# Down projections of a gated FFN by Strassen's seven block products, with written orders on three engines

## The chip, the cores and the metric

One Trainium2 chip, of which the kernel uses one core. Inside the core, TensorE multiplies matrices (a 128 x 128 block of weights is loaded, then up to 512 columns stream through it into a bank of PSUM), VectorE and GpSimd do elementwise work, ScalarE does activations and copies, and DMA queues move data between HBM and SBUF (here mostly the queue of SyncE). Only VectorE and ScalarE read PSUM here; GpSimd works on SBUF alone.

The metric is the device time of one execution in microseconds, as the median of the runs. Before the change it is 1626.29 us over three runs (1626.14 to 1626.61).

## The reference, cut to what matters

A trunk of two layers on 512 tokens with 1024 features: layer 0 mixes by dilated attention, layer 1 by a state space scan, and each is followed by the same gated FFN with 2816 hidden features. The change touches only the last product of the FFN:

```
def conv_ffn(h, w_up, conv_w, conv_b, w_down):
    u = causal_depthwise_conv(h @ w_up, conv_w, conv_b)
    gate, up = u[..., :D_FF], u[..., D_FF:]
    return (jax.nn.silu(gate) * up) @ w_down

for i in range(DEPTH):
    ...
    h = rmsnorm(x, ffn_norm_w[i])
    x = x + conv_ffn(h, ffn_w_up[i], ffn_conv_w[i], ffn_conv_b[i], ffn_w_down[i])
```

## The kernel before

**Layout and precision.** Features lie on the 128 partitions, tokens along the free dimension. The residual stream is eight tiles `xr[0..7]` of 128 x 512. Every operand of a large product is split into a high part (a cast to fp32r, on ScalarE) and a low part (value minus high part, on VectorE for weights, on GpSimd for the gated operands). `mm3` (line 136) then issues three products into one bank of PSUM: high weights by high operand, high by low, low by high. `in_turns` (line 129) only permutes the order in which columns stream.

**Loading.** `load_unit` (line 116) brings one 128 x 1024 block of weights: one DMA of 512 KB on SyncE's queue into a `raw` buffer (a ring of 4), the cast into `hi` (ScalarE), the difference into `lo` (VectorE). `hi` and `lo` have rings of 5, so units are prepared up to four ahead of TensorE.

**The FFN** (`ffn`, line 610) runs in three parts of 8, 8 and 6 tiles of hidden features (`FF_PARTS`). In each part an **up stage** goes over the tiles `c`. For the gate and the up half (`i = 2c`, `2c + 1`), `project` (line 146) makes 24 products of 512 columns into one of three `mm` banks; VectorE scales the bank by the row norm into `us` (line 620); `conv` (line 602) starts the three-tap convolution on ScalarE and adds two taps on VectorE. Then ScalarE takes the Silu of the gate half, GpSimd multiplies the halves (line 627), ScalarE casts the product and GpSimd takes the difference (line 630).

The **down block** follows: `down` (line 263) goes over the eight output tiles `m`; each has `cn` column blocks of weights in one loaded unit and `3 cn` products of 512 columns in one bank, after which VectorE adds the bank to `xr[m]` (line 640). The products that need the last hidden tile are put off (`held`, `late`), so that its convolution and split have time. Part 2 of layer 1 ends in `finish` (line 1059) instead, with the final norm; its last two output tiles are computed in halves of 256 tokens.

**What sets the order.** The scheduler of the framework orders each engine's instructions from a simulated timeline, except inside `tc.manual_schedule(engines=...)`: there the listed engines issue the block's instructions in the order of the program text. Where these fall among the same engine's instructions of outside the block stays with the scheduler. Before the change only TensorE's order is written in the down blocks. Other names that the steps below use: `aux_bank` (three banks of PSUM) and `side_bank` (two), `rbc` (the row norm along the free dimension), and `lp` and `k2`, the pools of SBUF tiles whose `tag` names a ring of buffers.

Of the kernel before, what the change touches and what calls it, by code (L numbers as in the profile page):

```python
# [51 lines left out]
def trunk(ctx: ExitStack, tc: tile.TileContext, A, out):  # L52
# [23 lines left out]
    def t2(name, tag, bufs, pool=k2, dtype=F32):  # L76
        return pool.tile([P, 512], dtype, tag=tag, name=name, bufs=bufs)
# [51 lines left out]
    def in_turns(ap):  # L129

        return ap.rearrange("p (a b f) -> p b a f", b=4, f=4)

    def long_product(dst, w, x, first, last):
        T.matmul(in_turns(dst), w, in_turns(x), start=first, stop=last)  # L134

    def mm3(dst, hi, lo, at, rh, rl, first, last):
        w_h = hi[:, at * P : (at + 1) * P]
        w_l = lo[:, at * P : (at + 1) * P]
        long_product(dst, w_h, rh, first, False)
        long_product(dst, w_h, rl, False, False)  # L140
        long_product(dst, w_l, rh, False, last)

    loaded = {}
    early = {}
# [457 lines left out]
    def conv(dst, src, c_w, c_b, taps):  # L602
        SC.activation(dst, src, AF.Identity, bias=col(c_b), scale=col(c_w + taps - 1))  # L603
        for j in range(1, taps):
            V.scalar_tensor_tensor(  # L605
                dst[:, j:], src[:, : S - j], col(c_w + taps - 1 - j), dst[:, j:],
                op0=ALU.mult, op1=ALU.add,
            )

    def ffn(layer, done):  # L610
        for part, (c0, cn) in enumerate(FF_PARTS):
            gh, gl = [], []
            for c in range(c0, c0 + cn):
                ab = []
                for gu in range(2):
                    i = 2 * c + gu
                    n = f"u{layer}_{i}"
                    p = project(A["wup"][layer * 44 + i], n)
                    us = t2("us" + n, "us", 3, lp)
                    V.tensor_tensor(us, p, rbc, op=ALU.mult)  # L620
                    a = t2("a" + n, "a", 13, lp)
                    conv(a, us, C_FCW + (layer * 44 + i) * 3, C_FCB + layer * 44 + i, 3)
                    ab.append(a)
                SC.activation(ab[0], ab[0], AF.Silu)

                by = V if layer == 1 and c == NFF - 1 else G
                by.tensor_tensor(ab[1], ab[0], ab[1], op=ALU.mult)  # L627
                g_h, g_l = high_low(f"g{c}")
                SC.copy(g_h, ab[1])
                by.tensor_tensor(g_l, ab[1], g_h.bitcast(F32), op=ALU.subtract)  # L630
                gh.append(g_h)
                gl.append(g_l)
            n = cn * P

            def load(m):
                i = (layer * len(FF_PARTS) + part) * KD + m
                return (*load_unit(A["wdn"][i][:, :n], f"wd{i}", n), 0)

            def add(m, p):
                V.tensor_tensor(xr[m], xr[m], p, op=ALU.add)  # L640
                if part == len(FF_PARTS) - 1:
                    done(m)

            if layer == 1 and part == len(FF_PARTS) - 1:
                finish(load, lambda c: (gh[c], gl[c]), cn)
                return
            with tc.manual_schedule(engines={mybir.EngineType.PE}):
                down(f"wd{layer}{part}", load, range(KD), lambda c: (gh[c], gl[c]), cn, add, late=True)

    def ups(layer, some):  # L650
        return [(A["wup"][layer * 44 + i], f"u{layer}_{i}") for i in some]
# [524 lines left out]
def _layout(i):  # L1176

    a = {k: np.asarray(v) for k, v in i.items()}
    f = np.float32
    xt = a["x"].reshape(S, D).T  # L1180
    xp = xt.reshape(D, P, DIL).transpose(0, 2, 1).reshape(KD, P, S)
    w = {"xt": xt.reshape(KD, P, S), "xp": xp}
    qkv = a["attn_w_qkv"][0].reshape(KD, P, NG, 3, NH, HD)
    qk = qkv[:, :, :, :2].transpose(4, 2, 3, 1, 0, 5).reshape(NH, 6, P, D)
    v0 = qkv[:, :, 0, 2].transpose(2, 1, 0, 3).reshape(NH, 1, P, D)
    w["wqk"] = np.concatenate([qk, v0], 1).reshape(56, P, D)
    w["wv"] = (
        qkv[:, :, 1:, 2].reshape(4, 2, P, 2, 2, 512).transpose(3, 4, 0, 2, 1, 5).reshape(16, P, D)
    )
# [5 lines left out]
    wdn = np.zeros((2, len(FF_PARTS), KD, P, 8, P), f)  # L1195
    for part, (c0, cn) in enumerate(FF_PARTS):
        wdn[:, part, :, :, :cn] = dn[:, c0 : c0 + cn].transpose(0, 3, 2, 1, 4)
    w["wdn"] = wdn.reshape(-1, P, 1024)
# [24 lines left out]
    return w  # L1223
# [22 lines left out]
```

## Time and profile before

| | |
|---|---|
| median of 3 runs | 1626.29 us (1626.14 to 1626.61) |
| the profiled execution | 1626.55 us |
| its span in the profile | 1624.6 us |
| mean granted clock of TensorE | 0.999 |
| read from HBM over the span | 161.62 MB |

The profile comes from one execution, so sums made from its rows stand against 1626.55 us. Its views name engines by short names: PE is TensorE, PEld its loads of weights, DVE VectorE, ACT ScalarE, POOL GpSimd, SP or SPq the queue of SyncE. A row of a group gives the source line, engine, operation, output and inputs by the names of the program, shapes and count, then total busy time and mean duration, then the idle time of the engine just before these instructions and what ended it. A row of the timeline gives the start in us from the start of the span, the duration, and the instruction. Matmuls are pipelined: the duration of one is longer than the distance from one to the next, which is what counts. Busy time of an engine is no limit of itself; it must be read stage by stage.

### The profile page before, as it was taken

The page shows a single profiled execution, that of the slowest core. Times are in us where ns is not written, and L with a number is a line of the kernel's source. Part 1 is how long each engine was busy: PE and PEld are TensorE (multiplying, and loading weights), DVE is VectorE, ACT ScalarE, POOL GpSimd, SP SyncE. Part 2 cuts the span into 40 slices and gives each one's busy share as a digit, 9 for nine tenths or more (in the row PEclk, how much of TensorE's full clock was granted, in tenths as well). Part 3 has the DMA queues.
Part 4 walks back from the last instruction along what each step waited for, and adds up shares of the span by engine and source line. Part 5 has one row for each costly group of instructions (what it writes and reads, how often), then busy time and mean ns, then how long its engine had stood idle before and what let it go on. Part 6 is the DMA issues. An engine that isn't in the chain of part 4 may idle for free.

```text
span 1624.6 us, 21067 instructions
## 1 busy us (share of the span) xinstructions
PE 1615.7 (99%) x8038; PEld 1382.9 (85%) x8038; DVE 1082.8 (67%) x1813; ACT 655.0 (40%) x965; POOL 418.6 (26%) x272
## 2 busy tenths in 40 slices
PE   9999999999999999999999999999999999999998
PEld 8888888888888888888887888888888888888887
DVE  6366665266647855764657899988897784574564
ACT  5233332333334532432445455544443442342343
POOL 0444453045402320220231222222111341121020
PEclk9999999999999999999999999999999999999999
DMA  7322222222224323223233433334332232332321
GB/s 259 98 80 83 78 91 80 96 85 79 78 78 134 113 91 105 103 81 117 81 101 104 148 108 115 100 100 127 114 126 90 93 104 91 104 104 91 104 78 52
DMA packets 53235, 165.13 MB, mean 102 GB/s; under 512 B 6224, under 2 KB 9680, under 8 KB 53136
## 3 DMA queue, kind: packets, MB, share of 16 engines
q1 hardware_dynamic: 52304, 163.01, 30.5%
q8 instruction: 63, 1.03, 0.3%
q10 hardware_dynamic: 832, 0.79, 0.1%
q14 instruction: 36, 0.29, 0.1%
HBM read 161.62 MB, written 2.16 MB: 101 GB/s over the span
## 4 chain that ended last, share of the span: by engine, by line
PE 99%; ACT 0%; DVE 0%; POOL 0%; POOLq 0%; DVEq 0%; issue 0%
PE u L134 29%; PE qk L134 16%; PE wd L134 12%; PE v L134 8%; PE xs L134 5%; PE z L134 5%; PE wso L134 5%; PE wo L134 3%; PE c L134 3%; PE b L134 3%; PE wz L134 2%; PE py L830 1%; PE pg L490 1%; PE pp L477 1%; PE po L485 1%; PE pf L838 1%
## 5 line engine op out<-in xcount | busy, mean ns | idle before, releaser
L134 PE MATMUL u<-xh,lo_u 128*128 128x512 f32 x704 | 268.9, 382 | 0.0
L134 PE MATMUL u<-xh,hi_u 128*128 128x512 f32 x704 | 268.8, 382 | 0.0
L134 PE MATMUL u<-xl,hi_u 128*128 128x512 f32 x704 | 266.3, 378 | 0.0
L627 POOL TENSOR_TENSOR au<-au,au 128x512 f32<-128x512 f32 x43 | 58.5, 1360 | 422.2 <-DVE au L605 396.6
L605 DVE SCALAR_TENSOR_TENSOR au<-usu,par,au 128x511 f32<-128x511 f32 (+1 forms) x176 | 159.4, 911 | 7.6 <-ACT au L603 2.9
L125 ACT CAST hi_u<-raw_u 128x1024 fp32r<-128x1024 f32 x88 | 91.1, 1044 | 168.4 <-PE u L134 95.6
L388 POOL TENSOR_TENSOR rotqk<-rotqk,sr 32x512 f32<-32x512 f32 x48 | 88.2, 1837 | 250.2 <-DVE rotqk L387 239.8
L134 PEld LDWEIGHTS u<-xl,hi_u 128*128 128x128 f32 x704 | 131.7, 187 | 24.5
L134 PEld LDWEIGHTS u<-xh,lo_u 128*128 128x128 f32 x704 | 131.7, 187 | 24.0
L134 PEld LDWEIGHTS u<-xh,hi_u 128*128 128x128 f32 x704 | 131.7, 187 | 21.8 <-issue 0.4
L134 PE MATMUL qk<-xh,hi_qk 128*128 128x512 f32 x384 | 148.6, 387 | 0.0
L134 PE MATMUL qk<-xh,lo_qk 128*128 128x512 f32 x384 | 147.1, 383 | 0.0
L134 PE MATMUL qk<-xl,hi_qk 128*128 128x512 f32 x384 | 145.6, 379 | 0.0
L126 DVE TENSOR_TENSOR lo_u<-raw_u,hi_u 128x1024 fp32r<-128x1024 f32 x88 | 113.8, 1299 | 29.9 <-ACT hi_u L125 29.9
L620 DVE TENSOR_TENSOR usu<-u,rbc 128x512 f32<-128x512 f32 x88 | 60.3, 690 | 93.1 <-PE u L134 86.4
L640 DVE TENSOR_TENSOR xr<-xr,wd 128x512 f32<-128x512 f32 x40 | 27.3, 688 | 116.9 <-PE wd L134 116.9
L125 ACT CAST hi_qk<-raw_qk 128x1024 fp32r<-128x1024 f32 x48 | 50.3, 1047 | 130.3 <-PE qk L134 69.3
L134 PEld LDWEIGHTS qk<-xh,lo_qk 128*128 128x128 f32 x384 | 71.8, 187 | 13.3
L134 PEld LDWEIGHTS qk<-xl,hi_qk 128*128 128x128 f32 x384 | 71.9, 187 | 12.8
L389 POOL TENSOR_TENSOR qk<-qk,rotqk 32x512 f32<-32x512 f32 x48 | 81.5, 1698 | 3.8
L125 ACT CAST hi_wd<-raw_wd 128x1024 fp32r<-128x1024 f32 (+1 forms) x48 | 46.1, 972 | 88.7 <-PE wd L134 55.6
L134 PEld LDWEIGHTS qk<-xh,hi_qk 128*128 128x128 f32 x384 | 71.9, 187 | 11.2
(647 smaller groups left out, 3768.5 us busy)
## 6 DMA issues: line engine op xcount, KB each, us to landing
raw_u<-in_wup SPq DMA_DIRECT2D x88, 512.0 KB, 3.3
raw_qk<-in_wqk SPq DMA_DIRECT2D x48, 512.0 KB, 3.3
raw_wd<-in_wdn SPq DMA_DIRECT2D x32, 512.0 KB, 3.2
raw_xs<-in_win SPq DMA_DIRECT2D x16, 512.0 KB, 3.3
raw_z<-in_win SPq DMA_DIRECT2D x16, 512.0 KB, 3.4
lm<-rows SPq DMA_DIRECT2D x32, 256.0 KB, 5.4
raw_wso<-in_wso SPq DMA_DIRECT2D x16, 512.0 KB, 3.3
raw_v<-in_wv SPq DMA_DIRECT2D x12, 512.0 KB, 3.5
```

What stands on the lines that cost most here:

```text
L125: SC.copy(hi[:, s], raw[:, s])
L126: low.tensor_tensor(lo[:, s], raw[:, s], hi.bitcast(F32)[:, s], op=ALU.subtract)
L134: T.matmul(in_turns(dst), w, in_turns(x), start=first, stop=last)
L388: G.tensor_tensor(rot[R, :], rot[R, :], sr[R, :], op=ALU.mult)
L389: G.tensor_tensor(at(t)[R], at(t)[R], of(rot)[R], op=ALU.add)
L477: T.transpose(pp[:, b * P : (b + 1) * P], pr[:, b * P : (b + 1) * P], ident)
L485: T.matmul(po[:, ii], v0[h][:, b * P : (b + 1) * P], pts[i][:, (b - i + 1) * P : (b - i + 2) * P], start=b == max(i - 1, 0), stop=b == i,)
L490: T.matmul(pg[:, ii], vt[g, half][i][:, es], pts[i][:, (g + 1) * P : (g + 2) * P], start=g == 1, stop=g == 2,)
L605: V.scalar_tensor_tensor(dst[:, j:], src[:, : S - j], col(c_w + taps - 1 - j), dst[:, j:], op0=ALU.mult, op1=ALU.add,)
L620: V.tensor_tensor(us, p, rbc, op=ALU.mult)
L627: by.tensor_tensor(ab[1], ab[0], ab[1], op=ALU.mult)
L640: V.tensor_tensor(xr[m], xr[m], p, op=ALU.add)
```

## The change

In parts 0 and 1 of both layers the down block is computed by a form of Strassen's scheme with 15 additions. The eight hidden tiles are taken in four pairs, the eight output tiles in four pairs (`mp`), the 512 tokens in two halves `H0` and `H1`. Instead of eight block products per pair, seven are made, with sums of weight blocks (`load_sevens`: `sums`, then `split_weights` of `a`, `b`, `c` with 1024 columns each and `d` with 512) and sums of operand halves (`split_first`, `split_second`, on GpSimd). Each block product is 128 x 128 by 256 columns, with the three products of `mm3` as before.

The results of the products are put together through `s1`, `s5`, `u`, `v` by ScalarE copies, VectorE adds from PSUM and GpSimd adds. Weights of the next row pair are prepared during the present one. Ahead of the block stand the two projections of the next part's first hidden tile (the **cover**, `held`): TensorE runs them while the last operands are split. The orders of TensorE, VectorE and ScalarE are written from the cover to the end of the block. Part 2 keeps the old block (its weights are laid out without padding now). The core of the diff:

```diff
+    def split_first(c, ga):
+        y = t2(f"y{c}", "a", 13, lp)
+        G.tensor_tensor(y[:, H0], ga[:, H1], ga[:, H0], op=ALU.subtract)
+        h, l = high_low(f"g{c}")
+        split_by(G, h[:, H0], l[:, H0], ga[:, H0])
+        split_by(G, h[:, H1], l[:, H1], y[:, H0])
+        return y, (h, l)
+    def split_second(c, ga, gb, y, j, fourth):
+        x = t2(f"x{c}", "a", 13, lp)
+        G.tensor_tensor(x[:, H0], gb[:, H1], y[:, H0], op=ALU.subtract)
+        G.tensor_tensor(y[:, H1], gb[:, H0], x[:, H0], op=ALU.subtract)
+        G.tensor_tensor(x[:, H1], gb[:, H1], ga[:, H1], op=ALU.subtract)
...
+        split_by(G, xhl[0][:, H0], xhl[1][:, H0], x[:, H0])
+        split_by(G, *f, y[:, H1])
+        b = split_whole(c, gb, G)
+        split_by(G, xhl[0][:, H1], xhl[1][:, H1], x[:, H1])
+        return xhl, f, b
+    def load_sevens(src, name):
...
+        dma(a[:, W0], src[:, 0:512])
+        dma(q, src[:, 512:1024])
+        dma(b[:, W1], src[:, 1024:1536])
+        dma(c[:, W0], src[:, 1536:2048])
+        def sums():
+            V.tensor_tensor(a[:, W1], q, b[:, W1], op=ALU.add)
+            V.tensor_tensor(b[:, W0], a[:, W1], a[:, W0], op=ALU.subtract)
+            V.tensor_tensor(c[:, W1], c[:, W0], b[:, W0], op=ALU.subtract)
+            V.tensor_tensor(q, a[:, W0], q, op=ALU.subtract)
+    def down_by_sevens(layer, part, pairs, cover, after):
...
+        sums, split_weights = load(0)
+        w = {}
+        sums()
+        w["a"] = split_weights("a")
+        src = [scaled(layer, 2 * cover)]
+        w["b"] = split_weights("b")
+        ab = [convolved(layer, 2 * cover, src[0])]
+        w["c"] = split_weights("c")
+        src.append(scaled(layer, 2 * cover + 1))
+        ab.append(convolved(layer, 2 * cover + 1, src[1]))
+        w["d"] = split_weights("d")
+        held = gate(layer, cover, ab)
+        for mp in range(KD // 2):
...
+            if not last:
+                sums, split_weights = load(mp + 1)
+            products(r1, w["a"], 0, lambda x, f, g0, g1: halves(g0, H0), True)
+            SC.copy(s1, r1)
+            if not last:
+                sums()
+                nxt["a"] = split_weights("a")
+            products(r3, w["a"], 4, lambda x, f, g0, g1: halves(g0, H1), True)
+            SC.copy(s5, r3)
+            G.tensor_tensor(low[:, H1], low[:, H1], s5, op=ALU.add)
+            products(r2, w["b"], 0, lambda x, f, g0, g1: halves(x, H0), True)
+            V.tensor_tensor(u, s1, r2, op=ALU.add)
+            G.tensor_tensor(top[:, H1], top[:, H1], u, op=ALU.add)
+            if not last:
+                nxt["b"] = split_weights("b")
+            else:
+                after(0)
+            products(r4, w["b"], 4, lambda x, f, g0, g1: f, True)
+            V.tensor_tensor(low[:, H0], low[:, H0], r4, op=ALU.add)
+            products(r1, w["c"], 0, lambda x, f, g0, g1: halves(g1, H0), False)
+            V.tensor_tensor(top[:, H0], top[:, H0], r1, op=ALU.add)
+            if not last:
+                nxt["c"] = split_weights("c")
+            else:
+                after(1)
+            products(r3, w["c"], 4, lambda x, f, g0, g1: halves(g1, H1), False)
+            V.tensor_tensor(top[:, H1], top[:, H1], r3, op=ALU.add)
+            products(r2, w["d"], 0, lambda x, f, g0, g1: halves(x, H1), False)
+            if not last:
+                nxt["d"] = split_weights("d")
+            V.tensor_tensor(v, s1, r2, op=ALU.add)
+            low3 = low.rearrange("p (h t) -> p h t", h=2)
+            G.tensor_tensor(low3, low3, v.unsqueeze(1).to_broadcast([P, 2, 256]), op=ALU.add)
...
+                for gu in range(2):
+                    fetch(2 * cover + gu)
+                E = mybir.EngineType
+                with tc.manual_schedule(engines={E.PE, E.DVE, E.Activation}):
+                    held = down_by_sevens(layer, part, pairs, cover, lambda i: fetch(2 * cover + 2 + i))
```

Per row pair `r1`, `r2`, `r4` are `aux` banks and `r3` a `side` bank; `r1`, `r2` and `r3` each take two of the seven products, one after the other, and are read between and after them. `fetch` is `load_unit` for one of the next up stage's blocks.

More of the change, by code (lines that the diff above doesn't have):

```diff
@@ L608, in conv, with up_name, scaled, convolved @@
             )
+    def up_name(layer, i):
+        return f"u{layer}_{i}"
+    def scaled(layer, i):
+        n = up_name(layer, i)
+        p = project(A["wup"][layer * 44 + i], n)
+        dst = t2("us" + n, "us", 3, lp) if i < 6 else p
+        V.tensor_tensor(dst, p, rbc, op=ALU.mult)
+        return dst
+    def convolved(layer, i, src):
+        a = t2("a" + up_name(layer, i), "a", 13, lp)
+        conv(a, src, C_FCW + (layer * 44 + i) * 3, C_FCB + layer * 44 + i, 3)
+        return a
+    def gate(layer, c, ab):
+        SC.activation(ab[0], ab[0], AF.Silu)
+        by = V if layer == 1 and c == NFF - 1 else G
+        by.tensor_tensor(ab[1], ab[0], ab[1], op=ALU.mult)
+        return ab[1], by
@@ new lines, in down_by_sevens, with load, products, halves @@
+    def down_by_sevens(layer, part, pairs, cover, after):
+        n = f"wd{layer}{part}"
+        def load(mp):
+            return load_sevens(A["wds"][(layer * 2 + part) * 4 + mp], f"{n}{mp}")
+        sums, split_weights = load(0)
[11 more added lines that the diff above has]
+        for mp in range(KD // 2):
+            last = mp == KD // 2 - 1
+            nxt = {}
+            r1, r3, r2, r4 = (
+                (side_bank if i == 1 else aux_bank)(f"{n}{mp}r{i}")[:, 0:256] for i in range(4)
+            )
+            top, low = xr[2 * mp], xr[2 * mp + 1]
+            kept_sums = t2("kept", "tmp", 2, lp)
+            both = t2("sums", "sq", 2)
+            s1, s5, u, v = kept_sums[:, H0], kept_sums[:, H1], both[:, H0], both[:, H1]
+            def products(dst, weights, at, operand, begin):
+                for j, pair in enumerate(pairs):
+                    mm3(
+                        dst, *weights, at + j, *(t for t in operand(*pair)),
+                        begin and j == 0, j == len(pairs) - 1, skip=True,
+                    )
+            def halves(t, h):
+                return [x[:, h] for x in t]
+            if not last:
[31 more added lines that the diff above has]
+            G.tensor_tensor(low3, low3, v.unsqueeze(1).to_broadcast([P, 2, 256]), op=ALU.add)
+            w = nxt
+        return held
@@ L610, in ffn, with fetch @@
     def ffn(layer, done):
+        held = None
         for part, (c0, cn) in enumerate(FF_PARTS):
-            gh, gl = [], []
+            gs = []
+            pairs, fourth = [], []
             for c in range(c0, c0 + cn):
-                ab = []
-                for gu in range(2):
[L616 to L632, printed above, removed]
+                g, by = held if c == c0 and held else gated(layer, c)
+                gs.append(g)
+                if part == len(FF_PARTS) - 1:
+                    pairs.append(split_whole(c, g, by))
+                elif c % 2 == 0:
+                    first = split_first(c, g)
+                else:
+                    y, g0 = first
+                    x, f, g1 = split_second(c, gs[-2], g, y, len(pairs), fourth)
+                    pairs.append((x, f, g0, g1))
+            if part < len(FF_PARTS) - 1:
+                cover = c0 + cn
+                def fetch(i):
+                    n = up_name(layer, i)
+                    loaded[n] = load_unit(A["wup"][layer * 44 + i], n)
+                for gu in range(2):
+                    fetch(2 * cover + gu)
+                E = mybir.EngineType
+                with tc.manual_schedule(engines={E.PE, E.DVE, E.Activation}):
+                    held = down_by_sevens(layer, part, pairs, cover, lambda i: fetch(2 * cover + 2 + i))
+                continue
@@ L633, in ffn @@
             n = cn * P
             def load(m):
-                i = (layer * len(FF_PARTS) + part) * KD + m
-                return (*load_unit(A["wdn"][i][:, :n], f"wd{i}", n), 0)
+                return (*load_unit(A["wdn"][layer * KD + m][:, :n], f"wd{layer}{m}", n), 0)
             def add(m, p):
                 V.tensor_tensor(xr[m], xr[m], p, op=ALU.add)
[L641 to L645, printed above, removed]
+                done(m)
@@ L646, in ffn @@
+            if layer == 1:
+                finish(load, lambda c: pairs[c], cn)
                 return
             with tc.manual_schedule(engines={mybir.EngineType.PE}):
-                down(f"wd{layer}{part}", load, range(KD), lambda c: (gh[c], gl[c]), cn, add, late=True)
+                down(f"wd{layer}{part}", load, range(KD), lambda c: pairs[c], cn, add, late=True)
     def ups(layer, some):
```

56 lines of the change are left out of this document (46 added, 10 removed).

## The prediction

> **What bounds the kernel now.** I read the page first, then the chain of waits in order of time, then the busy time by windows, then single instructions of the down projection and of the last, half-wide products. The page:
>
> ```profile
> span 1624.6 us, 21067 instructions
> PE 1615.7 (99%) x8038; PEld 1382.9 (85%) x8038; DVE 1082.8 (67%) x1813; ACT 655.0 (40%) x965; POOL 418.6 (26%) x272
> PE 99%; ACT 0%; DVE 0%; POOL 0%; POOLq 0%; DVEq 0%; issue 0%
> PE u L134 29%; PE qk L134 16%; PE wd L134 12%; PE v L134 8%; PE xs L134 5%; PE z L134 5%; PE wso L134 5%; PE wo L134 3%; PE c L134 3%; PE b L134 3%; PE wz L134 2%; PE py L830 1%; PE pg L490 1%; PE pp L477 1%; PE po L485 1%; PE pf L838 1%
> ```
>
> TensorE is 99% of the span and 99% of the chain: a microsecond of its products that goes away is a microsecond of time, as long as nobody else becomes late. `wd`, the products that the change touches, hold 12%. The chain in order of time shows the four touched blocks (parts 0 and 1 of each layer) and a stage between them:
>
> ```profile
> 588.36 42.24 PE wd L134 x192
> 630.60 84.48 PE u L134 x384
> 715.08 42.24 PE wd L134 x192
> 1349.98 42.24 PE wd L134 x192
> 1476.70 42.24 PE wd L134 x192
> ```
>
> Each block ends where the next begins (588.36 + 42.24 = 630.60): no gap to win, only products. One product of 512 columns costs 42.24 / 192 = 0.220 us. The windows of an up stage and of the down block behind it (us, then busy time and count of PE, PEld, DVE, ACT, POOL, then clock, DMA):
>
> ```profile
> core 0: us, PE busy (x) PEld busy (x) DVE busy (x) ACT busy (x) POOL busy (x), PEclk, DMA share, GB/s
> 502.80:588.30 85.50, 85.50 (x394) 72.53 (x393) 63.55 (x69) 40.64 (x53) 24.28 (x17) 1.00 0.33 111
> 588.30:630.60 42.30, 42.30 (x194) 35.96 (x193) 15.23 (x17) 9.41 (x11) 2.57 (x2) 1.00 0.26 88
> ```
>
> VectorE is busy 74% of the up stage and 36% of the down block, ScalarE 22% there, GpSimd 6%. The change spends just this room, so the question is whether it is enough.
>
> **What TensorE saves.** Per part the change has 4 row pairs x 7 products x 4 column pairs x 3 (high-high, high-low, low-high) = 336 products of 256 columns for 192 of 512. Products of 256 columns with the same access pattern stand in `finish`:
>
> ```profile
> 1607.94 0.27 PE L134 MATMUL wz<-g16h,hi_wd 128*128 128x256 f32 x1
> 1607.95 0.19 PEld L134 LDWEIGHTS wz<-g16l,hi_wd 128*128 128x128 f32 x1
> 1610.01 0.28 PE L134 MATMUL wz<-g16h,hi_wd 128*128 128x256 f32 x1
> 1611.98 0.28 PE L134 MATMUL wz<-g21h,lo_wd 128*128 128x256 f32 x1
> ```
>
> From the first to the last lie 35 steps in 4.04 us: 0.1154 us each, 5% more than half of 0.220. A load of weights takes 0.19 us but starts every 0.115 us beside the products, so it doesn't set the pace. Per part 336 x 0.1154 = 38.8 us, 3.47 us less; four parts save **13.9 us** (not the eighth of 169 us, 21, since narrow products are dearer). One of the seven products, 12 instructions, lasts 1.385 us, a row pair 9.69 us.
>
> **What is added on the other engines.** Their rows:
>
> ```profile
> 600.28 1.35 DVE L640 TENSOR_TENSOR xr<-xr,wd 128x512 f32<-128x512 f32 x2 [8.23 <-PE wd L134]
> 601.54 2.35 DVE L126 TENSOR_TENSOR lo_wd<-raw_wd,hi_wd 128x1024 fp32r<-128x1024 f32 x2
> 614.14 0.69 DVE L640 TENSOR_TENSOR xr<-xr,wd 128x512 f32<-128x512 f32 x1 [3.20 <-PE wd L134]
> 615.00 1.23 DVE L126 TENSOR_TENSOR lo_u<-raw_u,hi_u 128x1024 fp32r<-128x1024 f32 x1 [0.17 <-ACT hi_u L125]
> 1608.01 0.69 DVE L226 TENSOR_TENSOR ssum<-ssum,sq 128x512 f32<-128x512 f32 x1 [0.44 <-ACT sq L225]
> 1608.62 0.41 DVE L1076 TENSOR_TENSOR xr<-xr,wz 128x256 f32<-128x256 f32 x1
> L627 POOL TENSOR_TENSOR au<-au,au 128x512 f32<-128x512 f32 x43 | 58.5, 1360 | 422.2 <-DVE au L605 396.6
> L1096 POOL TENSOR_TENSOR ot<-xw,rbc 128x256 f32<-128x256 f32 x3 | 2.1, 729 | 1.4 <-ACT rbc L1114 1.4
> ```
>
> Instructions of VectorE that follow each other overlap a little: two of 1024 take 2.35, so the second adds 1.12; two of 512 add 1.26 until the next starts, 0.64 each (0.69 alone, SBUF or PSUM). For 256 I estimate 0.36 (0.41 less the same 0.05). A row pair then costs VectorE: `sums` 4 x 0.64 = 2.56, three splits of 1024 = 3.36, one of 512 = 0.64, five adds from PSUM of 256 = 1.8; together **8.4 us beside 9.69 us of TensorE**, where it had some 3.8. That alone fits. GpSimd gets `low += s5`, `top += u` (0.73 each) and `low3 += v` (1.29) per row pair, and in the up stage per pair of `c` 3 x 1.29 + 9 x 0.73 = 10.4 us of 21.1 (had 5.2). ScalarE's casts (some 3.7 us and two copies per row pair) have room. The bytes loaded stay (four loads of 256 KB for two of 512 KB per row pair, on SP); the ring of four `raw` buffers is refilled a row pair ahead, so I cost it at nothing; should that fail, the first sum waits for a load.
>
> **What stands between them.** VectorE and GpSimd disturb each other. Single instructions around the start of the first down block (580 to 594), then from the output projection of attention (489 to 500):
>
> ```profile
> 579.97 1.53 DVE L605 SCALAR_TENSOR_TENSOR au<-usu,par,au 128x511 f32<-128x511 f32 x2
> 583.98 1.23 DVE L126 TENSOR_TENSOR lo_wd<-raw_wd,hi_wd 128x1024 fp32r<-128x1024 f32 x1 [0.17 <-ACT hi_wd L125]
> 584.54 1.80 POOL L630 TENSOR_TENSOR g6l<-au,g6h 128x512 fp32r<-128x512 f32 x1 [1.62 <-ACT g6h L629]
> 585.29 2.39 DVE L605 SCALAR_TENSOR_TENSOR au<-usu,par,au 128x511 f32<-128x511 f32 x2
> 594.21 1.28 POOL L630 TENSOR_TENSOR g7l<-au,g7h 128x512 fp32r<-128x512 f32 x1 [0.73 <-ACT g7h L629]
> ...
> 489.28 1.54 POOL L226 TENSOR_TENSOR ssum<-ssum,sq 128x512 f32<-128x512 f32 x1 [38.37 <-ACT sq L225]
> 489.58 0.68 DVE L598 TENSOR_TENSOR xr<-xr,wo 128x512 f32<-128x512 f32 x1
> 490.18 1.72 DVE L126 TENSOR_TENSOR lo_wo<-raw_wo,hi_wo 128x1024 fp32r<-128x1024 f32 x1
> 500.45 2.30 DVE L126 TENSOR_TENSOR lo_u<-raw_u,hi_u 128x1024 fp32r<-128x1024 f32 x1
> ```
>
> GpSimd started under `lo_wd`, came on only when that ended at 585.21, and was done 1.13 us later; VectorE's pair behind it took 2.39 for 1.53. So a GpSimd instruction of 512 costs VectorE 0.86 us here, 0.49 in the 490.18 row and 1.07 in the 500.45 row (1.23 alone): I take **0.9**. An add that reads one operand from PSUM (489.58) keeps its 0.68 beside GpSimd. An instruction of 256 isn't shown; between 0 and 1.07 I take **0.35**: its 0.73 is 0.55 less than 1.28, and that comes off the 0.9. In the up stage VectorE then needs per pair of `c` 4 x (0.64 + 1.53 + 1.12) = 13.2 and at most 3 x 0.9 + 9 x 0.35 = 5.9, under 21.1: no stall of TensorE there; three banks of PSUM leave it two tiles of delay. In a row pair `top += u` falls beside adds from PSUM; `s5` and `v` cost 0.35 + 0.9: 8.4 + 1.25 = 9.65, barely inside 9.69.
>
> **The stall.** The written order of VectorE is late once, at the start. Rows for it:
>
> ```profile
> 588.40 0.69 DVE L620 TENSOR_TENSOR usu<-u,rbc 128x512 f32<-128x512 f32 x1 [0.72 <-PE u L134]
> L603 ACT ACTIVATE au<-usu,par 128x512 f32<-128x512 f32 x88 | 71.2, 813 | 1.9 <-DVE usu L620 1.4
> ```
>
> Time 0 is where the cover's two projections (2 x 24 x 0.220) end and the first product begins. At -5.08 VectorE scales the first cover tile (0.2 behind TensorE, as at 588.40), then split `b`, two convolution steps, split `c`: 0.64 + 1.12 + 1.5 + 1.12, to -0.7. GpSimd runs the last pair's half-wide operand steps just then, four of them in its way: +1.4, 0.7. Scale the second tile, 1.4; ScalarE 0.81, 2.25; two steps, 3.8; split `d`, 4.45; `sums` of the next row pair with the cover's gate on GpSimd in the way, 7.9; `s5` and split `a`, 9.4; only then `u`, 9.8. But the seventh product adds into the bank that `u` reads, and was due at 6 x 1.385 = 8.3. It waits 1.5 us; the next row pair's first product is queued behind it on TensorE, and needs the bank that `top += r1` frees after split `b` and two adds: 11.75 instead of 9.69. So **2.1 us** are lost there. ScalarE's copy of `s5`, queued behind the cast of `a`, holds the sixth product for less than that. From then on VectorE needs 9.65 us a row pair, 2.4 behind, and meets each due time (`u` 7.8 behind the start, due 8.3). The fourth row pair splits nothing for a fifth; the two `fetch` of up tiles (2 x 1.12) fit. The operands `x`, `f`, `g1` hold nobody: GpSimd's chain ends some 2 us behind time 0, the third product starts at 2.8, the last at 8.3.
>
> Without GpSimd in the way the same list gives 0.9 us, with full blocking 4.3 (below). I take 2.1, with the price that the rows show.
>
> **The sum.** The profiled execution took 1626.55 us (span 1624.6 and 1.95 around it), 0.26 above the median of 1626.29. 1626.55 - 13.9 + 4 x 2.1 = 1621.05; against the median 1620.8. I say **1621.0**, 0.33% faster. 0.2%, 3.25 us, is about what a measurement of this kernel can tell from no change.
>
> **Rivals.**
>
> No stall: 13.9 off, 1612.5. For it: 8.4 < 9.69. Against it: VectorE's order puts 4.7 us of work between the second cover tile and `u`. 6%.
>
> Cancelled: with the 1.07 of the 500.45 row, and so 0.5 for 256, the first loss is some 3 and each of the next two row pairs runs 0.3 over, 3.6 per part against 3.47 saved: 1626.5. 22%.
>
> The shared path decides, slower: each GpSimd instruction blocks VectorE for its whole length, 0.73 or 1.28. Then split `c` ends at 2.2, `u` at 12.05, the second row pair starts 4.3 late, and a row pair needs 8.4 + 1.28 + 0.73 = 10.4 for 9.69, 0.7 lost twice: 5.7 per part, 4 x 5.7 - 13.9 = +8.9, 1635.5. It turns slower where a part loses over 3.5. For it: the waiting in these rows is real, and the written order lets nothing pass; against: the costs shown are 0.49 to 1.07, not 1.28. With sums that cost 0.77, as the dependent convolution step does, and 1.07 for 256 too, it reaches some 7 per part, 1640. 27%. The Trainium skill ("SBUF — State Buffer", Who interferes with whom) states this rule: a VectorE instruction with two SBUF inputs and a GpSimd instruction that reads SBUF exclude each other for the whole instruction. The wait from 584.54 to 585.21 agrees with it, and so does the free add at 489.58; the price stays under the full length.
>
> Weight loads set the pace: 1344 x 0.19 = 255 us for 169, some 1712. The 35 steps at 0.1154 speak against it. 2%.
>
> The forecast, 0.9 to 2.6 us lost per part, has 43%: 1616 to 1623. Faster by over 0.2%: 43 + 6 = 49%; within 22%; slower 29%. The range, 1613 to 1640, leaves out the upper tail and the edge of the first rival.
>
> **What would show it.** Right: 336 narrow products per part at 0.115; one gap of TensorE per part ahead of the seventh product of the first row pair, released by VectorE's `u`, and one ahead of the second row pair's first, together 2 us; VectorE near 95% in the down block. Wrong: gaps in all row pairs (the lock), gaps in the up stage or behind the down block (tiles of `wup` fetched too late, split operands late), or narrow products slower than 0.12.

## The result, and the profile after

The changed kernel takes 1653.21 us (median of four runs, 1651.70 to 1654.66) against 1626.33 us for the one before. The ratio is 1.0165 (95% interval 1.0147 to 1.0183): **slower by 1.65%**, where the prediction said 0.33% faster and gave 1640 as the upper end. The profiled execution's span grew by 28.3 us. From the page of the kernel after, the span, the busy times and the shares of the chain that ended last:

```profile
span 1652.9 us, 22778 instructions
PE 1615.8 (98%) x8614; PEld 1403.8 (85%) x8614; DVE 1156.8 (70%) x1957; ACT 709.8 (43%) x1093; POOL 592.7 (36%) x448
PE 89%; DVE 5%; POOL 2%; ACT 1%; DMA 1%; issue 1%; SPq 0%; POOLq 0%; DVEq 0%; ACTq 0%
```

TensorE held 99% of the chain and now holds 89%. Its busy time did not fall either: matmuls that run at a lower clock take longer, which the rows below show. The chain in order of time, kernel after:

```profile
615.82 2.33 PE wd000r L134 x12
618.15 9.69 PE wd001r L134 x84
...
637.49 9.63 PE wd003r L134 x84
...
1271.32 1.32 PE u L134 x6
...
1328.65 39.87 PE u L134 x168
```

Row pairs two to four of the first block are dense and cost 9.63 to 9.69 us, as forecast. Of TensorE's work in the first row pair only the last of the seven products (12 instructions) is on the chain; ahead of it the chain runs through VectorE's list and through the load of `q`, the fourth weight tile (`DMA` 1%). Whether that load is the cause is what experiment 4 asks. TensorE's waits in the kernel after (what it waited for, us in total, times, longest):

```profile
PE u L134 <- DVE au L605: 8.5, 2, 6.7
PE wd110r L134 <- ACT kept L757: 3.2, 1, 3.2
...
PE wd010r L134 <- ACT kept L757: 2.9, 1, 2.9
PE wd100r L134 <- ACT kept L752: 1.5, 1, 1.5
```

`kept` L752 is ScalarE's copy of `s1`, L757 that of `s5`; names that end in `0r` are first row pairs. So there are two places: the first row pair of each block, and the up stages (`u`, two gaps). The first products of the first and the last block and of the row pairs behind them (count; shortest, median and longest in ns; first and last start):

```profile
L134 PE MATMUL wd000r<-g0h,hia_wd x2: 270/273/276, 601.2 to 602.5; 128*128 128x256 f32 x2
L134 PE MATMUL wd001r<-g0h,hia_wd x2: 279/280/280, 618.0 to 619.4; 128*128 128x256 f32 x2
L134 PE MATMUL wd110r<-g8h,hia_wd x2: 270/273/276, 1511.0 to 1512.4; 128*128 128x256 f32 x2
L134 PE MATMUL wd111r<-g8h,hia_wd x2: 271/314/357, 1528.5 to 1529.9; 128*128 128x256 f32 x2
```

A first row pair lasts 618.0 - 601.2 = 16.8 us here and 17.5 in the last block; the other two have 16.4 and 17.4. **The account**: four blocks of 4 x 9.63 instead of 42.24 save 14.9. First row pairs cost 68.1 for 38.5, 29.6 lost; their aftermath in the second ones 1.4. In layer 0 the first block starts at 601.2 instead of 588.36 + 10.56 for the moved cover: 2.3. In layer 1 the first up products (1271.32 against 1262.14) are 9.2 late and the block (1378.9 against 1349.98 + 10.56) 18.4, so 9.2 were lost between. 29.6 + 1.4 + 2.3 + 9.2 - 14.9 = 27.6 of the 28.3. Of the 29.6, 19.7 are idle time: TensorE is busy 48.4 us in the four first row pairs, 9.9 more than the 38.5 of dense products, which is the lower clock behind their gaps (last section).

**The first row pair.** Single instructions of layer 0, part 0, in the kernel after, by engine (VectorE, ScalarE, GpSimd, the SP queue, TensorE):

```profile
593.87 0.68 DVE L693 TENSOR_TENSOR rawa_wd<-q_wd,rawb_wd 128x512 f32<-128x512 f32 x1
594.59 1.66 DVE L694 TENSOR_TENSOR rawb_wd<-rawa_wd 128x512 f32<-128x512 f32 x1
599.41 1.35 DVE L640 TENSOR_TENSOR loa_wd<-rawa_wd,hia_wd 128x1024 fp32r<-128x1024 f32 x1 [0.88 <-ACT hia_wd L639]
600.68 0.69 DVE L618 TENSOR_TENSOR u<-u,rbc 128x512 f32<-128x512 f32 x1
610.77 0.93 DVE L693 TENSOR_TENSOR rawa_wd<-q_wd,rawb_wd 128x512 f32<-128x512 f32 x1 [1.56 <-DMA q_wd<-in_wds]
615.35 0.41 DVE L760 TENSOR_TENSOR sums<-kept,wd000r 128x256 f32<-128x256 f32 x1
...
611.73 1.04 ACT L639 CAST hia_wd<-rawa_wd 128x1024 fp32r<-128x1024 f32 x1 [3.46 <-DVE rawa_wd L693]
612.69 0.37 ACT L757 COPY kept<-wd000r 128x256 f32<-128x256 f32 x1
...
594.09 1.60 POOL L630 TENSOR_TENSOR au<-au,au 128x512 f32<-128x512 f32 x1 [5.75 <-DVE au L605]
...
605.59 0.33 SPq L687 DMA_DIRECT2D rawa_wd<-in_wds  x1
606.01 1.34 SPq L688 DMA_DIRECT2D q_wd<-in_wds  x3
...
613.10 0.39 PE L134 MATMUL wd000r<-g1h,hic_wd 128*128 128x256 f32 x1 [3.12 <-ACT kept L757]
```

VectorE works through its instructions in the written order; call the stretch that ends in `u` its list. The list begins with scaling the first cover tile. The prediction put that at -5.08, counted from the first product of the block; here it stands at 600.68 - 601.2 = -0.5. Ahead of it stand the first row pair's own `sums` (from 593.87) and split `a` (to 600.76), which the prediction took as done long before. The list is 4.6 us late, so ScalarE's cast of `a` is, and the copy of `s5` queued behind it; `u` ends at +14.6 where 9.8 was forecast. On top, the second `sums` wait 1.56 us for the fourth weight tile `q`: it lies in the ring of 13 that also holds the convolution outputs and operand sums, and its load sits in SP's queue behind `rawa` of a later row pair (605.59, then 606.01).

### The profile page after: what moved, and what is told of

It is laid out like the page before. It is cut to its first block, busy times and chain, and to the rows that moved or that the text cites. A ratio compares the mean times of both kernels' runs of the same rounds, so it can differ in the third digit from the quotient of the medians.

```text
span 1652.9 us, 22778 instructions
## 1 busy us (share of the span) xinstructions
PE 1615.8 (98%) x8614; PEld 1403.8 (85%) x8614; DVE 1156.8 (70%) x1957; ACT 709.8 (43%) x1093; POOL 592.7 (36%) x448
## 4 chain that ended last, share of the span: by engine, by line
PE 89%; DVE 5%; POOL 2%; ACT 1%; DMA 1%; issue 1%; SPq 0%; POOLq 0%; DVEq 0%; ACTq 0%
PE u L134 23%; PE qk L134 15%; PE v L134 8%; PE xs L134 5%; PE z L134 5%; PE wso L134 5%; PE wo L134 3%; PE c L134 3%; PE b L134 3%; PE wz L134 2%; PE wd L134 2%; DVE au L605 2%; DMA q_wd<-in_wds 1%; PE py L1009 1%; PE pg L490 1%; POOL au L630 1%
## 5 line engine op out<-in xcount | busy, mean ns | idle before, releaser
L134 PE MATMUL u<-xh,hi_u 128*128 128x512 f32 x704 | 270.3, 384 | 8.5 <-DVE au L605 8.5
L134 PE MATMUL u<-xh,lo_u 128*128 128x512 f32 x704 | 269.9, 384 | 0.0
L134 PE MATMUL u<-xl,hi_u 128*128 128x512 f32 x704 | 267.4, 380 | 0.0
L134 PEld LDWEIGHTS u<-xh,hi_u 128*128 128x128 f32 x704 | 132.3, 188 | 31.0 <-ACT hi_u L125 9.3
L134 PEld LDWEIGHTS u<-xl,hi_u 128*128 128x128 f32 x704 | 132.3, 188 | 24.5
L134 PEld LDWEIGHTS u<-xh,lo_u 128*128 128x128 f32 x704 | 132.2, 188 | 24.5
L134 PE MATMUL qk<-xh,hi_qk 128*128 128x512 f32 x384 | 148.7, 387 | 0.0
L134 PE MATMUL qk<-xh,lo_qk 128*128 128x512 f32 x384 | 147.2, 383 | 0.0
L134 PE MATMUL qk<-xl,hi_qk 128*128 128x512 f32 x384 | 145.7, 379 | 0.0
L605 DVE SCALAR_TENSOR_TENSOR au<-u,par,au 128x510 f32<-128x510 f32 (+1 forms) x152 | 113.5, 748 | 34.0 <-ACT au L603 30.3
L618 DVE TENSOR_TENSOR u<-u,rbc 128x512 f32<-128x512 f32 x76 | 53.0, 697 | 102.3 <-PE u L134 102.3
L954 POOL TENSOR_TENSOR xdd<-xdt,dec 128x384 f32<-128x384 f32 x16 | 18.0, 1140 | 241.2 <-DVE xdt L953 241.2
L384 DVE TENSOR_TENSOR qk<-qk,cr 128x512 f32<-128x512 f32 x48 | 33.0, 688 | 72.7 <-PE qk L134 72.5
L134 PEld LDWEIGHTS qk<-xh,lo_qk 128*128 128x128 f32 x384 | 71.8, 187 | 13.3
L134 PEld LDWEIGHTS qk<-xl,hi_qk 128*128 128x128 f32 x384 | 71.9, 187 | 12.8
L126 DVE TENSOR_TENSOR lo_qk<-raw_qk,hi_qk 128x1024 fp32r<-128x1024 f32 x48 | 59.3, 1236 | 31.9 <-ACT hi_qk L125 31.9
L134 PEld LDWEIGHTS qk<-xh,hi_qk 128*128 128x128 f32 x384 | 71.9, 187 | 11.3
```

The source lines that it names most:

```text
L126: low.tensor_tensor(lo[:, s], raw[:, s], hi.bitcast(F32)[:, s], op=ALU.subtract)
L384: V.tensor_tensor(at(t), of(p), of(cr), op=ALU.mult)
L605: V.scalar_tensor_tensor(dst[:, j:], src[:, : S - j], col(c_w + taps - 1 - j), dst[:, j:], op0=ALU.mult, op1=ALU.add,)
L618: V.tensor_tensor(dst, p, rbc, op=ALU.mult)
L954: G.tensor_tensor(v4(u[:, 0:384], 3), v4(t[:, 0:384], 3), b3(dec3[:, 0:3, heads[x]], 64), op=ALU.mult)
```

## The experiments

All ratios are against the kernel before, run beside the others on the same chip. **Theory A**: the first sums, and so VectorE's list, were put late because `q`'s buffer comes late. **Theory B**: ScalarE's order, the copies behind casts, is the cost. **Theory D**: in the up stages a bank of PSUM is held by a tile that was scaled in place, behind a GpSimd that is late.

**1. A ring of its own for the fourth weight tile.**

```diff
-        q = t2(f"q_{name}", "a", 13, lp)
+        q = t2(f"q_{name}", "us", 3, lp)
```

> Only q, the fourth weight tile of a row pair, changes its ring of buffers: from the 13 of tag a, which the up stage holds full, to the 3 of tag us, which are free after the sixth unit. Its loads can then start early, and the sums and the split of a move ahead of the cover in VectorE's order. Theory A (VectorE's written chain from the cover to u sets the first row pair, and it starts some 5 us late because q's buffer comes late): the first row pair of each block, 16.9, 16.5, 17.5 and 17.5 us in the changed kernel, falls to 11.5 to 13; the other row pairs stay 9.65; total 1653 - 4 x 5 = about 1633. Theory B (ScalarE's order: the copies s1 and s5 stand behind the cover's convolution and the cast of a): the waits ahead of the fifth and sixth product stay as they are, 1.5 and 3 us, total 1648 or more. Theory C (the shared path of VectorE and GpSimd alone): no change beyond 2 us. The up stages of part 0 keep their gaps of 1.8 and 6.7 us by all three.

Measured: 1633.33 us, ratio 1.0040 (1.0021 to 1.0060), 19.9 us less than the changed kernel. VectorE's rows of this kernel:

```profile
570.90 0.68 DVE L693 TENSOR_TENSOR rawa_wd<-q_wd,rawb_wd 128x512 f32<-128x512 f32 x1
...
584.29 1.23 DVE L640 TENSOR_TENSOR loa_wd<-rawa_wd,hia_wd 128x1024 fp32r<-128x1024 f32 x1 [1.09 <-ACT hia_wd L639]
...
595.65 0.70 DVE L618 TENSOR_TENSOR u<-u,rbc 128x512 f32<-128x512 f32 x1 [0.63 <-PE u L134]
...
611.95 0.41 DVE L760 TENSOR_TENSOR sums<-kept,wd000r 128x256 f32<-128x256 f32 x1
```

The first sums move from 593.87 to 570.90, deep into the up stage, split `a` from 599.41 to 584.29, and the list starts 5.05 us ahead of the first product (600.7). First row pairs take 13.2, 11.3, 11.7 and 11.3 us: 9.0 us lost over four blocks. In three of them that is 1.7 to 2.1 us each, and TensorE waits only for `u` there (1.0 to 1.5); in the first it is 3.6, where a wait of 1.5 for `s5` stands as well and `u` ends at +11.7. The total is what theory A expected. The waits for `s1` (L752, 1.5 us per block in the changed kernel) are gone in all four.

**2. The copy of `s5` ahead of the sums and the cast of `a`.**

```diff
             SC.copy(s1, r1)
-            if not last:
-                sums()
-                nxt["a"] = split_weights("a")
             products(r3, w["a"], 4, lambda x, f, g0, g1: halves(g0, H1), True)
             SC.copy(s5, r3)
             G.tensor_tensor(low[:, H1], low[:, H1], s5, op=ALU.add)
+            if not last:
+                sums()
+                nxt["a"] = split_weights("a")
```

> Only the place in the text of the copy s5 and of low += s5 changes: ahead of the next row pair's sums and cast of a, so that ScalarE no longer holds s5 behind that cast. VectorE's order stays. Theory B (ScalarE's order is the cost): the sixth product starts at once, its 3.1 us gap and the half clock behind it go, 4 x 4 = 16 us less, about 1637. Theory A (VectorE's u is what the block waits for): the gap moves from the sixth to the seventh product, which then waits some 4 us for u instead of 0.4; total within 4 us of 1653.

Measured: 1653.50 us, ratio 1.0165 (1.0136 to 1.0195), no gain. TensorE's waits of this kernel:

```profile
PE wd100r L134 <- DVE sums L760: 4.3, 1, 4.3
```

The waits for `s5` are gone, and 3.8 to 4.3 us per block stand later as a wait for `u`. The name in the largest wait was not the cause; it was the first consumer of a late list. Theory B falls for `s5`. For `s1`, whose waits stay here, it falls by experiment 1, which leaves ScalarE's written order as it was and has none of them.

**3. The cover's convolutions and gate in the last row pair.**

```diff
-        ab = [convolved(layer, 2 * cover, src[0])]
...
-        ab.append(convolved(layer, 2 * cover + 1, src[1]))
-        held = gate(layer, cover, ab)
...
+            if last:
+                held = gate(layer, cover, [convolved(layer, 2 * cover + i, src[i]) for i in range(2)])
```

> The convolution of the cover's two tiles and its gate go from ahead of the first row pair to the last row pair, where VectorE splits no weights: 3 us of VectorE and one product of GpSimd less in the crowded place. q's ring stays as in the changed kernel. Theory A, with q's load landing at 610.7 as before (its issue stands behind another load that waits for the split of c): VectorE comes free some 2 us earlier but then waits for that load, so the first row pair falls from 16.9 by at most 2, total 1645 to 1651. If the load weren't binding, it would fall by 3.5 to 4, total about 1638. Theory B: the copy s1 no longer stands behind the convolution, 1.5 us less per block, 1647.

Measured: 1629.38 us, ratio 1.0016 (1.0005 to 1.0028), first row pairs of 10.9 to 11.0. A miss: the gain was far larger than expected. With fewer tiles in the ring of 13 the loads also changed places, so this run alone doesn't part the shorter list from the earlier loads. The row of the SP queue in this kernel, where all four `q` of a block leave at once:

```profile
578.90 1.85 SPq L688 DMA_DIRECT2D q_wd<-in_wds  x4
```

The first sums still stand at 593.99. So a late list can be mended in two ways: start it earlier (1), or take four convolution steps and the activations between them out of it.

**4. The loads' order written too.** To part the order from the loads:

```diff
-                with tc.manual_schedule(engines={E.PE, E.DVE, E.Activation}):
+                with tc.manual_schedule(engines={E.PE, E.DVE, E.Activation, E.SP}):
```

> The order of SP's loads in the down blocks is written down too; the order of VectorE's instructions stays what it was, the first sums still stand behind the last up tile's convolution. Theory A1 (what costs most is the place that the first sums and split a got in VectorE's order; the late load of the fourth tile of the second row pair adds its own wait, 1.6 us at the second sums): only that wait goes, and the s5 wait shrinks from 3.1 to some 1.5, with less of the half clock behind it: 1.6 to 3 us per block, 1641 to 1647. Theory A2 (the loads as they arrive are the whole cause): first row pairs of 11 to 13 us as with the ring of its own, 1633. Theory A3 (loads don't matter at run time): 1653.

Measured: 1656.12 us, ratio 1.0180 (1.0166 to 1.0194). Nothing is won; the 1641 to 1647 of theory A1 is a miss, and A3 comes nearest. Rows of the SP queue and of VectorE in this kernel:

```profile
564.32 0.33 SPq L688 DMA_DIRECT2D q_wd<-in_wds  x1
...
593.45 0.68 DVE L693 TENSOR_TENSOR rawa_wd<-q_wd,rawb_wd 128x512 f32<-128x512 f32 x1
...
610.26 1.77 DVE L693 TENSOR_TENSOR rawa_wd<-q_wd,rawb_wd 128x512 f32<-128x512 f32 x1
...
615.67 0.41 DVE L760 TENSOR_TENSOR sums<-kept,wd000r 128x256 f32<-128x256 f32 x1
```

The second sums no longer wait for `q`, but `u` still starts at 615.67 (615.35 after the change): other waits filled the 1.56 us (those for `s1` grew from 1.5 to 2.5 in each block). The first `q` leaves at 564.32, 14 us earlier than in the changed kernel (578.70), and still the first sums stand at 593.45. So the late load is not a cost at run time by itself, and the first `q` lacks no buffer at run time either. What the ring of 13 did was done when the order was made: with `q` in it the first sums stand 23 us later in VectorE's order (593.87 against 570.90). That the simulated timeline had the ring full there is the likely reason; no run shows that timeline.

**5. Experiments 1 and 3 together.**

> Both edits that shortened the first row pairs together: the fourth weight tile in a ring of its own, and the cover's convolutions and gate in the last row pair. Theory A (a first row pair is late because VectorE's list of it starts late, and the list starts late because the first sums stand behind the fourth tile's load): with the moved convolutions 1.1 us per block were left, in front of u; with the first sums done under the up stage the list starts some 4.6 us earlier and u is early: first row pairs 9.7 instead of 10.9, 4 x 1.2 = 4.8 less than 1629.4, so 1624 to 1626; the gaps of the first up stages stay (2 and some 8.6 us). Rival B (u is late because sums of the next row pair and split a stand before it in the written order, wherever the list starts): first row pairs stay at 10.9, 1629 to 1630.

Measured: 1623.49 us, ratio 0.9983 (0.9974 to 0.9993), **0.17% under the kernel before**, about as little as can be told from no change. The chain of this kernel:

```profile
606.16 4.63 PE wd000r L134 x38
610.79 9.69 PE wd001r L134 x84
...
724.34 9.63 PE wd010r L134 x84
```

First row pairs are as dense as the others, but for 0.5 us in one block (10.4). `u` stood behind sums and split `a` in the same order and was in time: that is theory A, and it speaks against rival B of that text.

**6. `u` ahead of split `a`** (with 3 and 8: late convolutions, and GpSimd's part of the first two `c` on VectorE; the copy of `s5` moves ahead of the sums as in 2).

```diff
             if not last:
                 sums()
-                nxt["a"] = split_weights("a")
...
             V.tensor_tensor(u, s1, r2, op=ALU.add)
             G.tensor_tensor(top[:, H1], top[:, H1], u, op=ALU.add)
             if not last:
+                nxt["a"] = split_weights("a")
                 nxt["b"] = split_weights("b")
```

> Three edits: the cover's convolutions and gate in the last row pair; in every row pair u before split a and the copy of s5 before the sums of the next row pair; GpSimd's part of the first two c of each layer on VectorE. Theory A: the 1.1 us in front of u go, since 1.8 us of split a come behind it; split a comes some 2 us later, which is early enough for the next row pair: first row pairs 9.7 to 9.9, 4 x 1.1 = 4.4 less than 1629.4, and 3.6 less in the up stages as measured for that part alone: 1621 to 1622. Rival: u still waits for the sums ahead of it, or what stood behind split a is late instead: 1625 to 1627.

Measured: 1631.89 us, ratio 1.0039 (1.0024 to 1.0053), slower than either part led to expect. TensorE's waits of this kernel:

```profile
PE wd001r L134 <- DVE xr L766: 1.6, 1, 1.6
...
PE wd013r L134 <- DVE xr L766: 0.4, 1, 0.4
```

L766 adds `r4` to the residual. Now splits `a` and `b` stand together ahead of it, the next row pair waits for that add, and every row pair pays (11.4 to 11.5 us for the first, 10.2 to 10.3 for the two behind it). Moving one step, with VectorE at its limit, moved the wait.

**7. All scaled tiles in SBUF**, to test theory D.

```diff
-        dst = t2("us" + n, "us", 3, lp) if i < 6 else p
+        dst = t2("us" + n, "us", 3, lp)
```

> Only the place of the scaled up tiles goes back to SBUF, for all tiles as in the kernel before, instead of in place in the PSUM bank. Theory D (the gaps of 2 and 6.7 us in the first up stage of each layer come because a bank is held until the convolution has read it, and the convolution stands behind casts that wait for GpSimd): the gaps ahead of u go, 9 to 11 us less, 1641 to 1645; the first row pairs keep their 16 to 17.5 us. Rival E (GpSimd and the casts behind it are late by themselves, and TensorE waits for that wherever the tiles lie): gaps of the same size, 1650 to 1655. Rival F (two SBUF inputs of all convolution steps beside twice as many GpSimd instructions make VectorE the bound in the up stages): many small gaps in the second up stages too, over 1660.

Measured: 1656.04 us, ratio 1.0181 (1.0166 to 1.0196). The two gaps ahead of `u` are gone, as theory D says, yet nothing is won (it expected 1641 to 1645). A new wait, ahead of a block's first product:

```profile
PE wd100r L134 <- ACT hia_wd L639: 3.9, 1, 3.9
```

The lateness came back ahead of the blocks, and first row pairs grew to 17.8 to 20.0 us.

**8. GpSimd's part of the first two `c` of each layer on VectorE.**

```diff
-        by = V if layer == 1 and c == NFF - 1 else G
+        by = V if c < 2 or layer == 1 and c == NFF - 1 else G
```

`split_first` and `split_second` take the same choice.

> For the first pair of hidden tiles of each layer (c = 0 and 1) GpSimd's work, the gate's product and all sums and differences of operands, goes to VectorE. Theory D (in the first up stage of a layer GpSimd falls behind, 17 us for that pair, ScalarE's queue waits for its results, the convolutions behind them hold the three banks of PSUM that now keep the scaled tiles, and TensorE runs out of banks): the gaps of 1.8 us (layer 0) and 6.7 us (layer 1) go, with the half clock behind the second: 1653 - 10 = 1643. Theory E (VectorE itself is behind there after the row norm): more work for VectorE makes the gaps longer, 1656 or more. The down blocks stay as they are.

Measured: 1649.65 us, ratio 1.0141 (1.0106 to 1.0177), 3.6 less than the changed kernel by the medians. That size is not clear of noise: the two runs took 1652.11 and 1647.19. The profile is that of the slower one; in it the gap of layer 0 went, and that of layer 1 fell from 6.7 to 4.7 us. The expected 1643 is a miss.

**9 to 11. Both causes of the up stage, on experiment 5**: twelve units in SBUF instead of six, GpSimd's relief, and both.

> The fourth weight tile in a ring of its own, the cover's convolutions in the last row pair, and the scaled tiles of the first 12 units of a layer in SBUF (6 before), so that no bank is held while GpSimd is behind; later units stay in place in PSUM, the covers too. Theory D (the bank that is held makes the gap): both gaps ahead of u go, 1.8 and 6.5 us and the half clock behind the second: 1623.5 less 9 to 11, 1612.5 to 1615, which is all of the 13.9 that narrower work saves. Rival E: the gap comes two units later, when banks are held again: 1619 to 1624. Rival F: with all convolution steps of the first pairs on two SBUF inputs VectorE gets late and the first down block with it: 1618 to 1626.

> The fourth field of a two by two: ring of its own and late convolutions, GpSimd's part of the first two c of each layer on VectorE, but only the first 6 units in SBUF. Measured so far: neither 1623.5, 12 units in SBUF alone 1623.7, both 1616.4. Theory G (GpSimd's own lateness in the first pair is the root; the held bank and the late operands of the down block are two places where it shows): GpSimd's relief alone brings most of it, 1616 to 1619, with what is left a gap in layer 1. Rival D (a held bank is a cost by itself, and needs the tiles in SBUF): the gap of some 4.7 us in layer 1 stays with its half clock, 1619.5 to 1621.

> The run before with GpSimd's part of the first two c of each layer on VectorE. If the gaps are gone already, nothing is left to win: 1613 to 1616; if VectorE (whose load in these stages rises by some 13 us) becomes late, a gap in the first up stages: 1616 to 1622.

| | first 6 units in SBUF | first 12 |
|---|---|---|
| GpSimd as in the change | 1623.49 (0.9974 to 0.9993) | 1623.71 (0.9975 to 0.9993) |
| first two `c` relieved | 1618.05 (0.9936 to 0.9964) | 1616.44 (0.9928 to 0.9953) |

In brackets is the interval of the ratio to the kernel before. TensorE's waits, first with twelve units in SBUF alone, then with both:

```profile
PE u L134 <- DVE au L605: 3.8, 2, 2.5
PE wd000r L134 <- POOL x7l L640: 2.7, 1, 2.7
PE wd100r L134 <- POOL x7l L640: 2.6, 1, 2.6
```

```profile
PE wd100r L134 <- POOL x7l L640: 2.6, 1, 2.6
...
PE u L134 <- DVE au L605: 0.5, 1, 0.5
```

Freeing the banks alone moves the wait to the last split operand (`x7l`) at the head of the block; so theory D's 1612.5 to 1615 is a miss. Relieving GpSimd takes 5.4 us away, and only then do the free banks bring 1.6 more; that step is at the edge of what these runs tell, since the two intervals overlap. GpSimd's lateness is the larger part, and the held bank decides where a lateness shows. It is not the whole: with the relief alone a gap of 4.8 us stays in layer 1, as rival D said, though the time lies in theory G's range. GpSimd has been idle for 28 us when that gap begins, while VectorE, which has its work now, shows no pause from 1284 to 1310. By these rows it is VectorE that is late there. The version with both, **0.6% faster than the kernel before**, is the best of the study. Against 1626.4 - 14.9 = 1611.5 it still lacks 5 us, of which 3.1 are the two waits shown; the rest was not followed up.

**12. Experiments 3, 6, 7 and 8 together.**

> The three edits of the run before and the scaled up tiles in SBUF. Theory A and D together: all gaps but the chain of the row norm go; 1626.3 - 13.9 + 0.3 to 3: 1613 to 1616. Rival E: the gap in layer 1 is not the bank's: 1620 to 1622. Rival F (convolution steps with two SBUF inputs make VectorE late): over 1626.

Measured: 1627.22 us, ratio 1.0005 (0.9996 to 1.0015). The gaps ahead of `u` are gone, and the 1.6 us of experiment 6 are there in all four blocks: a miss, by that step.

## Why the prediction was wrong

- **What TensorE saves**: right. 9.63 / 84 = 0.1146 us per narrow product; 14.9 us saved in dense products, 13.9 forecast.
- **VectorE's 9.65 us per row pair fit in 9.69**: right, with next to nothing to spare: row pairs two to four are dense, and in the second one VectorE is busy 9.53 us of 9.60 (618.20 to 627.80). The rival in which every row pair runs over did not happen.
- **The stall of 2.1 us per part**: the step that failed is its first line, "At -5.08 VectorE scales the first cover tile". It took the first `sums` and split `a` as done by then, though the diff puts them at the head of the same written list, and `q` into the ring of 13. They were not, the list began 4.6 us later, and the loss was 7.4 us per part (29.6 / 4), some 2.5 of it the lower clock (9.9 / 4), which the timetable doesn't have. Where experiment 1 makes the premise true (-5.05), the timetable holds in three blocks: `u` ends at 9.7 to 10.1 for the 9.8 forecast, and 1.7 to 2.1 us are lost for 2.1. The first block loses 3.6, with a wait for `s5` that the timetable doesn't have; so it is in part luck that the mean, 2.2, comes so near to 2.1.
- **The ring of weights ("so I cost it at nothing")**: wrong, but not by the wait for a load that the prediction named. Three of the four tiles lie in `raw`; the fourth lies in the ring of 13, which the diff shows and the prediction passed over. By experiments 1 and 4 that is where the late list comes from, through the order and not through the load.
- **"ScalarE's copy of `s5` ... holds the sixth product for less than that"**: wrong: it held the sixth product for 2.9 to 3.2 us, as a result of the late list (experiment 2). With the list on time it holds it for 1.5 in one block and not at all in three (experiment 1). The copy of `s1`, which held the fifth product for 1.5 us in each block, is not in the prediction.
- **"no stall of TensorE there; three banks of PSUM leave it two tiles of delay"** (the up stage): wrong, 2.3 and 9.2 us. GpSimd's operand steps were added up at undisturbed durations, 10.4 us for a pair of `c`, and the disturbance was charged to VectorE alone. Also, the diff scales units from the seventh on in place, so a bank is free only after the last convolution step; the delay of two tiles was not there. The gaps come only in the first up stage of a layer, which starts behind the row norm: in layer 1 three tiles stand ready when VectorE scales the first one at 1299.63. The kernel before has the same backlog there (at 1290.45) and no gap.
- **Where the sum comes out**: put the first row pairs right (experiment 1) and add the up stages, and the forecast's 1621.0 becomes 1621.0 + 2.3 + 9.2 = 1632.5, against 1633.3 measured in experiment 1. That it comes so near has some luck in it: 1.0 us more was saved than forecast, and 0.6 more lost in the first row pairs.
- The range ended at 1640 because its slow rival was the shared path of VectorE and GpSimd at full price in the block. The mechanism that did decide, the place of the first sums, was not among the rivals.

GpSimd and ScalarE in the first up stage of layer 1, kernel after, and the product that waited:

```profile
1306.09 1.29 POOL L630 TENSOR_TENSOR au<-au,au 128x512 f32<-128x512 f32 x1 [12.11 <-DVE au L605]
1307.46 1.60 POOL L650 TENSOR_TENSOR y<-au 128x256 f32<-128x256 f32 x1
1309.01 1.18 POOL L640 TENSOR_TENSOR g0l<-au,g0h 128x256 fp32r<-128x256 f32 x1
...
1319.88 2.90 POOL L640 TENSOR_TENSOR x1l<-x,x1h 128x256 fp32r<-128x256 f32 x2
1322.74 0.72 POOL L640 TENSOR_TENSOR f1l<-y,f1h 128x256 fp32r<-128x256 f32 x1
1323.42 1.26 POOL L630 TENSOR_TENSOR au<-au,au 128x512 f32<-128x512 f32 x1
...
1324.71 0.40 ACT L639 CAST g2h<-au 128x256 fp32r<-128x256 f32 x1 [3.83 <-POOL au L630]
1325.02 1.44 ACT L603 ACTIVATE au<-u,par 128x512 f32<-128x512 f32 x2
...
1328.65 0.76 PE L134 MATMUL u<-xh,hi_u 128*128 128x512 f32 x1 [6.72 <-DVE au L605]
```

An instruction of 256 that takes 0.72 undisturbed takes 1.18, 1.45 (2.90 for two) or 1.60. The twelve steps of one pair, from 1306.09 to 1323.46, came to 15.9 us of work for the 10.4 forecast. The next multiplication starts late for it, ScalarE's cast waits 3.83 us for that, the convolution's activation `1325.02` stands behind the cast although its own input was ready, and the in-place bank is released only when VectorE's steps follow.

## What to carry to other kernels

When an order is written by hand for a stretch, look first at what stands at its head: what must come in before the first instruction, and from which ring its buffers come. Here the ring of one tile fixed the place of the whole list when the order was made, and an earlier load did not bring it back. A late list shows in a profile under the name of its first impatient consumer; moving that consumer only renamed the wait. And where two engines disturb each other, charge both of them.

## What the runs showed of the hardware

**The disturbance goes both ways, and lasts to the end of the other's instruction.** `rawb<-rawa` (594.59) takes 1.66 us for 0.69: GpSimd's multiplication runs until 595.69, and VectorE ends 0.56 later. That multiplication itself takes 1.60 for 1.28, since it met `sums` L693, which ends at 594.55. The Trainium skill ("SBUF — State Buffer", the section on SBUF's two separate sides) calls the shared pair an exclusive lock that whoever starts first keeps for the whole instruction; these rows agree with that. The 0.9 that the prediction charged to VectorE for a GpSimd instruction of 512 was a fair price for its side (0.97 here), with GpSimd's 0.32 missing.

**A gap of 3 us costs more than itself.** Windows behind the 3.12 us gap and behind the 6.72 us gap, kernel after (us, busy time and count of PE, PEld, DVE, ACT, POOL, then clock, DMA):

```profile
613.10:616.00 2.90, 2.47 (x13) 2.17 (x14) 2.90 (x5) 2.47 (x3) 1.38 (x2) 0.63 0.00 0
...
1329.00:1332.00 3.00, 3.00 (x8) 2.32 (x8) 1.29 (x2) 0.77 (x3) 2.62 (x2) 0.50 0.24 53
```

The granted clock is 0.63 in the 2.9 us behind the gap of 3.12, and 0.50 behind that of 6.72, where eight products of 512 take 3.0 us for 1.76. Behind the gap of 1.51 in the same row pair it is 1.00 (the 12 products between 608.30 and 613.10). The length of the gap alone doesn't set it: behind the 2.89 us of the second block it is 0.53 (743.40 to 746.30). The lower clock is why TensorE's busy time stayed at 1615.8 although 14.9 us of products went: 9.9 came back in the first row pairs, 1.4 in the second ones, and 2.9 in the row `1328.65 39.87 PE u L134 x168` (168 x 0.220 = 37.0). The Trainium skill ("TensorE: Matmul & The Clock Gate", Why this matters for your kernels) warns of idle gaps above some 3 us; this trace agrees. In experiment 1, where the gaps in the blocks are 1.0 to 1.5 us, the mean clock is 0.997, against 0.991 in experiment 2, where they reach 3.8 to 4.3; the gap of 6.7 in the up stage stands in both.
